# Splitting the weights of the projections beside the forgetting attention during the dense stage and keeping the two parts in DRAM

## The chip, the cores and the metric

One Trainium2 chip, one core. The metric is the device time of one launch in microseconds (us), the median of several runs. All matrix work is fp32 in and out.

## The reference

One residual block over 1024 tokens of width 1024. After an RMS norm a combined input projection feeds three token mixers: a gated linear recurrence (HGRN2), a forgetting attention (8 heads of 64 with a cumulative log-forget bias), and a cross-attention into 256 memory tokens. Three sigmoid gates of width 1024 weigh the three branches, one output projection closes the mixer, and a ConvGLU feed-forward layer follows. The lines that bear on the change:

```python
z = h @ w_in[l].astype(jnp.float32)
(hq, hf, hi, hg, fq, fk, fv, ff, mq, gate_logits) = jnp.split(z, pts, axis=-1)
y_a = _hgrn2_mixer(hq, hf, hi, hg, lower_bounds[l], hgrn_norm_g[l])
y_b = _fox_mixer(fq, fk, fv, ff, fox_f_bias[l], fox_q_norm_g[l], fox_k_norm_g[l])
...
y_c = _memory_mixer(mq, mem_kv, mem_q_norm_g[l], mem_k_norm_g[l])
gates = jax.nn.sigmoid(gate_logits).reshape(B, T, N_BRANCH, D_MODEL)
merged = (gates[:, :, 0] * (y_a @ w_br_hgrn[l].astype(jnp.float32))
          + gates[:, :, 1] * (y_b @ w_br_fox[l].astype(jnp.float32))
          + gates[:, :, 2] * (y_c @ w_br_mem[l].astype(jnp.float32)))
```

## The kernel before

**Split operands.** TensorE (PE) multiplies in a one-pass fp32 form (fp32r). To keep fp32 accuracy each operand is split in a high part, which is the value cast to fp32r, and a low part, which is the value minus the high part. A product then takes three matmuls (`mm3`, L248 to L250; in the attention stage L1229): high by high, high by low, low by high. The split of a weight tile is a cast on ScalarE (ACT, helper line L254) and a subtraction on VectorE (DVE, helper line L262, or L1216 in the attention stage). The raw weights come from DRAM into the tiles `raw` (two buffers) or `rw` (two buffers, dense stage); the parts lie in `wh` and `wl` (`WIDE` = 4 buffers each).

**Stages.** In the profile's time: start and memory keys (0 to 80 us); the dense stage (80 to about 250 us), in which 20 chunks of 128 output channels of the input projection (four for the memory queries, sixteen for gates) are made in ten pairs; values and first queries and keys of the attention, woven with the memory attention (to about 371 us); the attention stage (371 to 674 us); HGRN2; the merge and the output projection; the feed-forward layer from about 1000 us.

**Dense stage.** `dense_unit` makes one pair with seven block products instead of eight, from the four blocks a11, a21, a22, a12 of the pair's weights and their sums (L662). `Dense.open` issues the two loads of `rw` on GpSimd's queue (POOL, L684) when the unit begins and splits the first operands; `Dense.operand` makes each split on ACT and DVE. A tile scheduler puts the instructions of each engine in order ahead of time; on the chip each engine takes its own in that order. SP issues the stores of the gates (L770) and the loads of the tiles `raw`.

**Attention stage.** Here a planner, class `Plan`, writes the order of all engines out by hand: chains of work name an engine, a cost and the time from which they can start, and the planner takes the chain that can start first, lower rank first. `rows` makes logits and softmax (L1085, L1086, L1099, L1120), `outcomes` transposes the weights of attention, splits them (`ph`, `pl`, L254 and L1161) and multiplies with the values (L1171, L1172), `pairs` makes the next head pair's queries and keys. `fill`, with the lowest rank, fills PE with projections that have nothing to do with the attention heads at hand (L1229): first a job with the weights of head pair 1, then four parts of `w_late[0]` (queries and keys of head pairs 2 and 3), four gate chunks of `w_cm`, four parts of `w_late[1]` (HGRN2's inputs), and three chunks of `w_cm` for HGRN2's head 0. The 15 weight tiles of these last jobs, 128 x 1024 each, go through `stage_weights`: a load on SP's queue (L1207), then for each half a cast on ACT and a subtraction on DVE, as planned items between those of the attention:

```python
raw = wp.tile([P, 4 * 264], F32, tag="raw", name="raw", bufs=2)
t = yield "SP", 0.1, t
SP.dma_start(raw[:, :n], src[q] if count > 1 else src)
t += LOAD
...
for c in (slice(0, n // 2), slice(n // 2, n)):
    t = yield "ACT", act_us(n // 2), t
    cast(S, h[:, c], raw[:, c])
    t = yield "DVE", dve_us(n // 2), t + act_us(n // 2) + LAG
    V.tensor_sub(l[:, c], raw[:, c], h[:, c].bitcast(F32))
```

A slot of `wh` and `wl` comes free when the last matmul of an earlier job has read it (`ws.free`).

## Time and profile before

| | us |
|---|---|
| median of 3 runs | 1689.15 (1688.54 to 1690.55) |
| span of the profiled execution, first to last instruction | 1686.5 |
| the profiled execution's own time beside its span | not given apart; the median lies 2.6 above the span |
| PE busy | 1677.7 (99%) |
| DVE, ACT, POOL busy | 1170.4, 808.5, 326.6 |
| dense stage, 90 to 270: PE, DVE, ACT, POOL busy of 180 | 180.0, 102.4, 73.6, 7.5 |
| attention stage, 371 to 674: PE, DVE, ACT, POOL busy of 303 | 301.6, 226.7, 185.6, 143.4 |
| granted TensorE clock | 1.000 |

Matmuls are pipelined: one of 512 columns is listed with about 0.39 us but the next one starts 0.227 us later. So "busy" does not tell whether PE runs at its own pace; the distance from one matmul's start to the next does. In rows of the timeline the columns are start and duration in us, engine, line, operation, output and inputs, shape, count, and in brackets the engine's idle time before it and what ended it.

### The profile page before, as it was taken

What the parts mean: (1) busy time and instruction counts of PE and PEld (TensorE: products, weight loads), DVE (VectorE), ACT (ScalarE), POOL (GpSimd) and SP (SyncE); (2) the same over time, 40 slices, a digit from 0 to 9 for tenths busy, and PEclk for the clock granted to TensorE, in tenths of its full rate; (3) what the DMA queues carried; (4) which work ended last, traced back from release to release, by engine and by line L of the source; (5) the groups of instructions that cost most, each with busy time, mean ns of one, the idle gap of its engine ahead of it and who ended that gap; (6) DMA issues with size and microseconds to landing.
All of it is one profiled execution on the core that took longest, in us unless ns stands there. A gap on an engine that the chain in (4) does not pass through costs nothing.

```text
span 1686.5 us, 23254 instructions
## 1 busy us (share of the span) xinstructions
PE 1677.7 (99%) x8409; PEld 1415.8 (84%) x8409; DVE 1170.4 (69%) x2118; ACT 808.5 (48%) x1459; POOL 326.6 (19%) x430
## 2 busy tenths in 40 slices
PE   9999999999999999999999999999999999999999
PEld 7888889998888888888888888888888888888887
DVE  6966554558688766766856745988788888775664
ACT  6734444656576556666521333634344444533432
POOL 0200001336464423433201000211111111100000
PEclk9999999999999999999999999999999999999999
DMA  9442324122142233100337641666454454494782
GB/s 376 171 145 105 118 77 157 71 100 69 57 133 87 75 101 101 51 20 19 107 106 257 207 151 58 189 180 182 132 144 131 122 166 132 176 352 154 239 283 88
DMA packets 87348, 235.50 MB, mean 140 GB/s; under 512 B 9904, under 2 KB 12600, under 8 KB 87104
## 3 DMA queue, kind: packets, MB, share of 16 engines
q1 hardware_dynamic: 68032, 166.83, 28.4%
q0 software_dynamic: 18624, 66.59, 13.9%
q8 instruction: 66, 1.08, 0.3%
q10 hardware_dynamic: 576, 0.59, 0.1%
q14 instruction: 50, 0.41, 0.1%
HBM read 184.91 MB, written 72.13 MB: 152 GB/s over the span
## 4 chain that ended last, share of the span: by engine, by line
PE 96%; DVE 2%; ACT 1%; DMA 1%; issue 0%; ACTq 0%; DVEq 0%
PE pp L250 17%; PE pp L249 17%; PE pp L248 17%; PE pp L1229 10%; PE lg L248 5%; PE lg L250 5%; PE lg L249 5%; PE tr L250 3%; PE tr L249 3%; PE tr L248 3%; PE tr L1147 2%; PE po L1172 1%; PE lg L1085 1%; PE lg L1086 1%; PE po L248 1%; PE po L249 1%
## 5 line engine op out<-in xcount | busy, mean ns | idle before, releaser
L254 ACT CAST wh<-s 128x512 fp32r<-128x512 f32 x122 | 73.3, 620 | 133.1 <-PE pp L249 73.3
L254 ACT CAST wh<-rw 128x512 fp32r<-128x512 f32 x96 | 58.5, 619 | 113.8 <-PE pp L249 69.7
L254 ACT CAST wh<-raw 128x512 fp32r<-128x512 f32 (+2 forms) x85 | 63.9, 756 | 96.0 <-PE pp L249 76.3
L254 ACT CAST dwh<-wr 128x1024 fp32r<-128x1024 f32 (+1 forms) x41 | 40.2, 980 | 114.1 <-PE tr L249 37.6
L250 PE MATMUL pp<-uh,wl 128*128 128x512 f32 x224 | 89.0, 397 | 0.0
L248 PE MATMUL pp<-uh,wh 128*128 128x512 f32 x224 | 88.8, 396 | 0.0
L249 PE MATMUL pp<-ul,wh 128*128 128x512 f32 x224 | 88.4, 395 | 0.0
L1161 DVE TENSOR_TENSOR pl<-tr,ph 128x512 fp32r<-128x512 f32 (+1 forms) x96 | 51.4, 551 | 30.7 <-ACT ph L254 30.3
L1120 ACT ACTIVATE pt<-pt,st 128x128 f32<-128x128 f32 (+3 forms) x64 | 49.6, 775 | 45.9 <-DVE st L1116 30.6
L1229 PE MATMUL pp<-wl,uh 128*128 128x512 f32 (+1 forms) x192 | 70.0, 365 | 0.0
L1229 PE MATMUL pp<-wh,uh 128*128 128x512 f32 (+1 forms) x192 | 69.5, 362 | 0.0
L1229 PE MATMUL pp<-wh,ul 128*128 128x512 f32 (+1 forms) x192 | 69.4, 362 | 0.0
L262 DVE TENSOR_TENSOR dwl<-wr,dwh 128x1024 fp32r<-128x1024 f32 (+1 forms) x41 | 46.3, 1130 | 30.5 <-ACT dwh L254 30.5
L254 ACT CAST ph<-tr 128x512 fp32r<-128x512 f32 (+1 forms) x96 | 44.2, 477 | 41.0 <-PE tr L1147 39.6
L1124 POOL TENSOR_SCALAR pt<-pt,st 128x128 f32<-128x128 f32 (+3 forms) x64 | 52.0, 815 | 60.1 <-DVE st L1122 58.4
L1828 POOL DMA_DIRECT2D rw<-in_w_up x42 | 23.2, 558 | 200.0 <-DVE wl L1718 190.1
L1718 DVE TENSOR_TENSOR wl<-rw,wh 128x512 fp32r<-128x512 f32 x69 | 46.6, 687 | 21.2 <-PE pp L250 17.9
L1718 DVE TENSOR_TENSOR wl<-s,wh 128x512 fp32r<-128x512 f32 x85 | 57.9, 683 | 0.0
L262 DVE TENSOR_TENSOR wl<-raw,wh 128x512 fp32r<-128x512 f32 (+2 forms) x54 | 52.1, 964 | 7.0 <-ACT wh L254 7.0
L248 PE MATMUL pp<-wh,uh 128*128 128x256 f32 (+1 forms) x192 | 55.2, 287 | 0.0
L250 PE MATMUL pp<-wh,ul 128*128 128x256 f32 (+1 forms) x192 | 55.0, 286 | 0.0
L249 PE MATMUL pp<-wl,uh 128*128 128x256 f32 (+1 forms) x192 | 54.4, 283 | 0.0
(520 smaller groups left out, 5602.2 us busy)
## 6 DMA issues: line engine op xcount, KB each, us to landing
rw<-in_w_up POOLq DMA_DIRECT2D x42, 512.0 KB, 4.8
sd<-in_w_dn POOLq DMA_DIRECT2D x30, 512.0 KB, 6.0
br<-yd SPq DMA_DIRECT2D x30, 512.0 KB, 5.6
gd<-gt SPq DMA_DIRECT2D x48, 256.0 KB, 2.0
gt<-gd SPq DMA_DIRECT2D x48, 256.0 KB, 2.8
yd<-fc SPq DMA_DIRECT2D x44, 256.0 KB, 2.8
wr<-sd SPq DMA_DIRECT2D x20, 512.0 KB, 4.9
raw<-in_w_cm SPq DMA_DIRECT2D x18, 512.0 KB, 3.5
```

The lines of the kernel that those rows point to most:

```text
L248: PE.matmul(ps, lh, rh, start=first, stop=False, skip_group_check=more)
L249: PE.matmul(ps, lh, rl, start=False, stop=False, skip_group_check=more)
L250: return PE.matmul(ps, ll, rh, start=False, stop=last, skip_group_check=more)
L254: return S.copy(out, in_)
L262: return (sub or V).tensor_sub(l, src, h.bitcast(F32))
L1120: S.activation(pt, pt, AF.Exp, bias=st[:, 2:3], accum_out=st[:, 3:4])
L1124: G.tensor_scalar(pt, pt, st[:, 3:4], 0.0, ALU.mult, ALU.add)
L1147: PE.transpose(ptr[:, j * P:(j + 1) * P], pts[j][:, sb * P:(sb + 1) * P], ident)
L1161: V.tensor_sub(pl[:, c], ptr[:, c], ph[:, c].bitcast(F32))
L1229: PE.matmul(o, a, b, start=q == i == 0, stop=q == KC - 1 and i == 2)
L1718: late["split"] = V.tensor_sub(l, src, h.bitcast(F32))
L1828: late["raw"] = (SP if begun else G).dma_start(raw[:, 2 * i:2 * i + 2, :], src[:, 2 * i:2 * i + 2, :])
```

## The change

The 15 weight tiles of the projections in the attention stage are split earlier, in the dense stage, and both parts go to a DRAM tensor `wsd`. In the attention stage the two parts are loaded as they are.

- `stored_parts` is a generator that `dense_unit` advances four times in each unit but the first (at most one half tile each time). For each tile: the raw load on SP (L273), for each half a cast on POOL (L258, tile `piece`, two buffers in the places `ta` and `tb`), a subtraction on DVE that leaves the low part in `raw` (L262), a store of the high half (L743) and, after the second half, one of the low part (L745).
- `load_parts` issues two loads of 128 x 1024 on SP (L755), one into `wh`, one into `wl`. `stage_weights` only takes a free slot and calls it; the planner reckons with `LOAD` + 1.0.
- `Dense.load` issues a unit's weight loads on POOL (L678) one unit ahead, in the middle of the unit before, behind the last cast of a piece, and `open` uses what is there.
- In the dense stage and in the attention stage the scheduler and the planner come to another order on every engine; the numbers of instructions on PE and DVE stay as they were (8107 and 2120 in the program), ACT has 30 fewer, POOL 30 more, SP's queue 75 more.

```diff
+        def load(self, src):
+            self.ahead = self.raw()
+            for i in range(2):
+                G.dma_start(self.ahead[:, 2 * i:2 * i + 2, :], src[:, 2 * i:2 * i + 2, :])
+
         def open(self, src, places=None):
-            raw = []
-            whole = None if places else self.raw()
-            for i in range(2):
+            raw = [] if places else [self.ahead[:, i, :] for i in range(4)]
+            for i in range(2 if places else 0):
...
+    stored = [*((w_late, q) for q in range(4)), *((w_cm, 16 + 8 * br + j) for br, j in order[2 + NCOVER + NPAIR:]),
+              *((w_late, q) for q in range(4, 8)), *((w_cm, i) for i in (4, 0, 8))]
+    wsd = tc.dram_tile([len(stored), 2, P, T], F32, name="wsd")
+
+    def stored_parts():
...
+        fetch(0)
+        fetch(1)
+        yield
+        for i in range(len(stored)):
+            raw = raws.pop(i)[:, :T]
+            for n in range(2):
+                sl = slice(n * HB, (n + 1) * HB)
+                h = ps1.tile([P, HB], F32R, tag=("ta", "tb")[n], name="piece")
+                split(G, h, raw[:, sl].bitcast(F32R), raw[:, sl])
+                late["piece"] = late["split cast"]
+                SP.dma_start(wsd[i, 0][:, sl], h.bitcast(F32))
+                if n:
+                    SP.dma_start(wsd[i, 1], raw)
+                elif i:
+                    fetch(i + 1)
+                yield
+
+    def load_parts(i, shape):
+
+        n = shape[0] * shape[1]
+        hl = [wp.tile([P, 4 * 264], F32R, tag=g, name=g, bufs=WIDE) for g in ("wh", "wl")]
+        for c, t in enumerate(hl):
+            SP.dma_start(t[:, :n].bitcast(F32), wsd[i, c])
+        return [t[:, :n].rearrange("p (a b) -> p a b", a=shape[0]) for t in hl]
+
-    def dense_unit(src, put, first, families):
+    def dense_unit(src, put, first, families, spare, after):
...
         put(0, 1, y, e2)
+        next(spare, None)
+        if after is not None:
+            with tc.issue_after(late["piece"].ins) if "piece" in late else nullcontext():
+                dense.load(after)
...
-    ws, raws = Ring(WIDE, 2), Ring(2)
+    ws = Ring(WIDE, 2)
...
     def stage_weights(jobs):
-        for j, (src, shape, count) in enumerate(jobs):
+        at = 0
+        for j, (shape, count) in enumerate(jobs):
             parts[j] = []
             for q in range(count):
-                n = shape[0] * shape[1]
-                kr, t = yield from raws.get()
-                raw = wp.tile([P, 4 * 264], F32, tag="raw", name="raw", bufs=2)
-                t = yield "SP", 0.1, t
-                SP.dma_start(raw[:, :n], src[q] if count > 1 else src)
-                t += LOAD
-                kw, tw = yield from ws.get()
...
-                    cast(S, h[:, c], raw[:, c])
...
-                    V.tensor_sub(l[:, c], raw[:, c], h[:, c].bitcast(F32))
...
+                kw, t = yield from ws.get()
+                t = yield "SP", 0.2, t
+                parts[j].append((load_parts(at, shape), kw, t + LOAD + 1.0))
+                at += 1
```

**DVE at the passage from the first to the second dense unit, before.** `s1`, `s2`, `s3` and `s4` are block sums, `rw` the raw weights, `gt` evacuates a product from PSUM.

```order
L262 TENSOR_TENSOR wl_849<-s3_885,wh_848 128x512
L662 TENSOR_TENSOR s3_1003<-rw_923 128x512
L759 TENSOR_TENSOR gt_882<-lg_788,fe_845 128x512
L262 TENSOR_TENSOR wl_905<-rw_923,wh_904 128x512
L662 TENSOR_TENSOR s1_928<-rw_923 128x512
L662 TENSOR_TENSOR s2_934<-s1_928,rw_923 128x512
L757 SCALAR_TENSOR_TENSOR gt_901<-pp_787,fe_831 128x512
L262 TENSOR_TENSOR wl_931<-s1_928,wh_930 128x512
```

The same place now; `raw_1004` is the first of the 15 tiles.

```order
L262 TENSOR_TENSOR wl_850<-s3_889,wh_849 128x512
L662 TENSOR_TENSOR s3_1011<-rw_886 128x512
L807 TENSOR_TENSOR gt_883<-lg_789,fe_846 128x512
L262 TENSOR_TENSOR wl_909<-rw_886,wh_908 128x512
L262 TENSOR_TENSOR raw_1004<-raw_1004,piece_1030 128x512
L262 TENSOR_TENSOR raw_1004<-raw_1004,piece_1054 128x512
L662 TENSOR_TENSOR s1_929<-rw_886 128x512
L805 SCALAR_TENSOR_TENSOR gt_905<-pp_788,fe_832 128x512
L662 TENSOR_TENSOR s2_935<-s1_929,rw_886 128x512
L262 TENSOR_TENSOR wl_932<-s1_929,wh_931 128x512
```

Two subtractions, which wait for POOL's casts, now stand ahead of the sum `s1` and the low part `wl_932` that PE waits for.

**ACT in the attention stage before, where the second `w_late` group begins.** `ph` is a part of the transposed attention weights, `pt4` and `pt5` rows of the softmax, `kh` and `qa` keys and queries of the next head pair, `raw_5152` the group's first tile.

```order
L1000 ACTIVATE kh0_2_4872<-tr_5139,cv_71 64x512
L1000 ACTIVATE kh1_2_4873<-tr_5139,cv_71 64x512
L254 CAST ph_5174<-tr_5161 128x128
L254 CAST wh_5154<-raw_5152 128x512
L1120 ACTIVATE pt4_5178,st_5179<-pt4_5178,st_5179 128x640
L1186 COPY gt_5213<-po_5028 64x512
L1000 ACTIVATE qa0_2_4876<-tr_5210,fqs_185 64x512
```

ACT at the same keys and the same softmax row now.

```order
L1050 ACTIVATE kh0_2_5013<-tr_5286,cv_71 64x512
L1050 ACTIVATE kh1_2_5014<-tr_5286,cv_71 64x512
L1170 ACTIVATE pt4_5278,st_5279<-pt4_5278,st_5279 128x640
L254 CAST ph_5343<-tr_5317 128x384
L1317 ACTIVATE gt_5305<-gt_5305 128x512
L1170 ACTIVATE pt5_5329,st_5330<-pt5_5329,st_5330 128x768
```

The cast of the raw weights no longer stands between the keys and the softmax row.

**SP's queue in the attention stage, around the loads of the second `w_late` group and the gates' stores, before.** `gd` takes gates, `ybd` the attention's output, `z3_1` is a tile of queries and keys.

```order
L1281 DMA gd_197<-gt_5121 128x512
L1207 DMA raw_5152<-in_w_late 128x1024
L1321 DMA z3_1_5220<-zd_2248 128x4x256
L1192 DMA ybd_196<-gt_5213 64x512
L1281 DMA gd_197<-gt_5238 128x512
L1207 DMA raw_5367<-in_w_late 128x1024
```

The same part of the queue now; `wsd` holds the stored parts, and each load waits until PE has read the old content of its slot.

```order
L1319 DMA gd_197<-gt_5170 128x512
L755 DMA wh_5307<-wsd_706 128x1024
L755 DMA wl_5308<-wsd_706 128x1024
L1242 DMA ybd_196<-gt_5298 64x512
L1319 DMA gd_197<-gt_5305 128x512
L1359 DMA z3_1_5418<-zd_2414 128x4x256
```

Where one raw load (L1207) stood in SP's queue before, two loads of the same size stand now.

More of the change, by code (lines that the diff above doesn't have):

```diff
@@ L681, in open @@
                     t = t.rearrange("p (a b) -> p a b", a=2)
-                else:
-                    t = whole[:, 2 * i:2 * i + 2, :]
                 G.dma_start(t, src[:, 2 * i:2 * i + 2, :])
@@ L715, in tile_block, with fetch @@
     ps1 = home["sums"] = Rounded(tc, name="ps1", bufs=1, side="right", reuse_waits="tile")
-    def dense_unit(src, put, first, families):
+    stored = [*((w_late, q) for q in range(4)), *((w_cm, 16 + 8 * br + j) for br, j in order[2 + NCOVER + NPAIR:]),
+              *((w_late, q) for q in range(4, 8)), *((w_cm, i) for i in (4, 0, 8))]
+    wsd = tc.dram_tile([len(stored), 2, P, T], F32, name="wsd")
+    def stored_parts():
+        w_late_flat = [w_late[q // 4][q % 4] for q in range(8)]
+        raws = {}
+        def fetch(i):
+            if i < len(stored):
+                src, q = stored[i]
+                raws[i] = raw_weights(w_late_flat[q] if src is w_late else src[q], T)
+        fetch(0)
[21 more added lines that the diff above has]
+    def dense_unit(src, put, first, families, spare, after):
         raw, o1, o6, o2, s2, o3 = gen["unit"] if first else dense.open(src)
@@ L739, in dense_unit @@
         put(1, 1, x, e5)
+        next(spare, None)
         if not first:
@@ L743, in dense_unit @@
             put(0, 0, z, e1)
+            next(spare, None)
         product(x, dense.operand(a22), "T4", False)
         put(1, 0, x, None)
+        next(spare, None)
     def dense_put(chunks):
@@ L784, in tile_block @@
     run_all(cover)
+    spare = stored_parts()
     for i, chunks_of in enumerate(PAIRS):
-        dense_unit(w_pair[i], dense_put(chunks_of), i == 0, families)
+        dense_unit(w_pair[i], dense_put(chunks_of), i == 0, families, iter(()) if i == 0 else spare, w_pair[i + 1] if i + 1 < len(PAIRS) else None)
+    run_all(spare)
     home["raw"].release()
@@ L1199, in stage_weights @@
     def stage_weights(jobs):
-        for j, (src, shape, count) in enumerate(jobs):
+        at = 0
+        for j, (shape, count) in enumerate(jobs):
             parts[j] = []
             for q in range(count):
-                n = shape[0] * shape[1]
-                kr, t = yield from raws.get()
-                raw = wp.tile([P, 4 * 264], F32, tag="raw", name="raw", bufs=2)
-                t = yield "SP", 0.1, t
-                SP.dma_start(raw[:, :n], src[q] if count > 1 else src)
-                t += LOAD
-                kw, tw = yield from ws.get()
-                h, l = (wp.tile([P, 4 * 264], F32R, tag=g, name=g, bufs=WIDE) for g in ("wh", "wl"))
-                t = max(t, tw)
-                for c in (slice(0, n // 2), slice(n // 2, n)):
-                    t = yield "ACT", act_us(n // 2), t
-                    cast(S, h[:, c], raw[:, c])
-                    t = yield "DVE", dve_us(n // 2), t + act_us(n // 2) + LAG
-                    V.tensor_sub(l[:, c], raw[:, c], h[:, c].bitcast(F32))
-                    t += dve_us(n // 2) + LAG
-                raws.free(kr, t)
-                parts[j].append(([x[:, :n].rearrange("p (a b) -> p a b", a=shape[0]) for x in (h, l)], kw, t))
+                kw, t = yield from ws.get()
+                t = yield "SP", 0.2, t
+                parts[j].append((load_parts(at, shape), kw, t + LOAD + 1.0))
+                at += 1
     def three(ps, lh, ll, rh, rl):
@@ L1340, in tile_block @@
     gates = list(islice(early, NFOX))
-    sources = [(w_late[0], (2, HB), 4)] + [(w_cm[16 + 8 * order[i][0] + order[i][1]], (KC, P), 1) for i in gates]
-    sources += [(w_late[1], (2, HB), 4), *((w_cm[i], (KC, P), 1) for i in (4, 0, 8))]
+    sources = [((2, HB), 4), *[((KC, P), 1)] * NFOX, ((2, HB), 4), *[((KC, P), 1)] * 3]
     zr.update({(0, 0): 0.0, (0, 1): 7.0})
```

## The prediction

> **What bounds the kernel now.** I read the page's head first, then the windows of the two stages that the change touches, then PE's timeline in them.
>
> ```profile
> span 1686.5 us, 23254 instructions
> ...
> PE 1677.7 (99%) x8409; PEld 1415.8 (84%) x8409; DVE 1170.4 (69%) x2118; ACT 808.5 (48%) x1459; POOL 326.6 (19%) x430
> ```
>
> ```profile
> 90.00:270.00 180.00, 180.00 (x821) 150.10 (x820) 102.39 (x159) 73.56 (x128) 7.51 (x14) 1.00 0.30 105
> 371.00:674.00 303.00, 301.63 (x1661) 256.35 (x1661) 226.67 (x683) 185.63 (x384) 143.36 (x184) 1.00 0.29 95
> ```
>
> The columns of a window are its length, then PE, PEld, DVE, ACT and POOL busy, the granted clock, the DMA share and GB/s. PE has no idle time in the dense stage and 303.00 - 301.63 = 1.37 us in the attention stage, at a granted clock of 1.00. Busy alone proves little where a matmul is listed longer than its turn; the starts prove it:
>
> ```profile
> 177.01 0.39 PE L250 MATMUL tr<-uh,wl 128*128 128x512 f32 x1
> 177.24 0.39 PE L248 MATMUL tr<-uh,wh 128*128 128x512 f32 x1
> 177.47 0.39 PE L249 MATMUL tr<-ul,wh 128*128 128x512 f32 x1
> ```
>
> Matmuls of 512 columns follow each other every 0.23 us. The change leaves PE's instructions as they are, so it can only win where that distance is longer. In the attention stage these are the places where PE waits:
>
> ```profile
> 503.24 0.40 PE L1229 MATMUL pp<-uh,wl 128*128 128x512 f32 x1
> 504.02 0.50 PE L1085 MATMUL lg<-kh,qa 128*128 128x512 f32 x1 [0.38 <-DVE st L1099]
> ...
> 504.60 0.39 PE L1229 MATMUL pp<-uh,wh 128*128 128x512 f32 x1
> 505.13 0.41 PE L1085 MATMUL lg<-kh,qa 128*128 128x384 f32 x1
> ...
> 507.58 0.40 PE L1229 MATMUL pp<-uh,wh 128*128 128x512 f32 x1
> 508.09 0.50 PE L1085 MATMUL lg<-kh,qa 128*128 128x512 f32 x1
> ```
>
> ```profile
> 516.76 0.28 PE L1171 MATMUL po<-ph,vhl 128*128 128x256 f32 x1
> 517.57 0.39 PE L1172 MATMUL po<-pl,vhl 128*128 128x256 f32 x1 [0.53 <-DVE pl L1161]
> ```
>
> Less the turn (0.23, or 0.12 for 256 columns) they cost 0.55, 0.30, 0.28 and 0.69 us: **1.82 us** together. Three shorter ones stand earlier:
>
> ```profile
> 398.35 0.39 PE L1229 MATMUL pp<-wh,ul 128*128 128x512 f32 x1
> 398.87 0.30 PE L1085 MATMUL lg<-kh,qa 128*128 128x128 f32 x1
> ...
> 400.77 0.39 PE L1229 MATMUL pp<-wl,uh 128*128 128x512 f32 x1
> 401.13 0.50 PE L1085 MATMUL lg<-kh,qa 128*128 128x512 f32 x1
> ```
>
> ```profile
> 424.42 0.40 PE L1229 MATMUL pp<-wh,ul 128*128 128x512 f32 x1
> 424.90 0.63 PE L1147 MATMUL tr<-ident,pt 128*128 128x128 f32 x4
> ```
>
> They cost 0.29, 0.13 and 0.25 us. So all waits of this stage come to 2.5 us. After it I find two more that are worth naming, in HGRN2 and in the feed-forward layer:
>
> ```profile
> 695.79 0.22 PE L1511 MATMUL lg<-X 128*64 128x64 f32 x1
> 696.73 0.74 PE L1523 MATMUL lg<-X 128*128 128x64 f32 x5 [0.72 <-DVE X L1501]
> ```
>
> ```profile
> 1070.27 0.39 PE L249 MATMUL pp<-B11l,wh 128*128 128x512 f32 x1
> 1071.02 0.50 PE L250 MATMUL pp<-B11h,wl 128*128 128x512 f32 x1 [0.36 <-DVE wl L1718]
> ```
>
> By the starts, less a turn, they cost 0.83 and 0.52 us. With them the whole reserve behind the first matmuls is 2.5 + 1.35 = 3.85 us, 0.23% of the time.
>
> **What ends the waits.** The chain of waits goes from the matmuls of 504 to 508 us back through DVE and ACT to one load, and ACT's timeline shows it standing:
>
> ```profile
> 495.25 6.32 DMA raw<-in_w_late
> ```
>
> ```profile
> 501.60 0.62 ACT L254 CAST wh<-raw 128x512 fp32r<-128x512 f32 x1 [3.00 <-DMA raw<-in_w_late]
> ```
>
> ACT sits 3.00 us in front of the cast of a weight that PE does not need for a long time; the softmax row and the keys behind it are late, then DVE, then PE. The wait at 517.57 has another source of the same work:
>
> ```profile
> 515.05 2.13 DVE L1216 TENSOR_TENSOR wl<-raw,wh 128x512 fp32r<-128x512 f32 x2
> ```
>
> Two subtractions of weights stand ahead of `pl` and take 2.13 us together instead of about 1.3.
>
> **The change, removed.** From ACT's and DVE's order in the attention stage go 30 casts and 30 subtractions:
>
> ```profile
> L1216 DVE TENSOR_TENSOR wl<-raw,wh 128x512 fp32r<-128x512 f32 x30 | 22.6, 759 | 1.9 <-ACT wh L254 1.8
> ```
>
> That is 22.6 us of DVE's 226.7; the 30 casts at the 0.62 us of the row at 501.60 are 18.6 us of ACT's 185.6. On a stage that PE sets, this is worth nothing in itself: 303 us of PE turns stay. What goes with it is the cause of the four waits: neither ACT nor DVE meets a weight load any more. I take 1.82 us, with the bounds 0 (other lateness takes the same places) and 2.5 (every wait of the stage goes).
>
> **Moved to the dense stage.** 30 casts on POOL. The nearest row has the same shape:
>
> ```profile
> L258 POOL TENSOR_SCALAR vhl<-Vf x8: 620/622/1586, 375.8 to 597.5; 128x512 fp32r<-128x512 f32 x8
> ```
>
> 30 x 0.62 = 18.6 us on an engine with 7.5 of 180 us busy. The 30 subtractions at about 0.69 us, the duration of the rows below, are 20.7 us more on DVE, 102 + 21 = 123 of 180. What covers it is the lead that the splits have over PE:
>
> ```profile
> 168.44 0.69 DVE L262 TENSOR_TENSOR wl<-rw,wh 128x512 fp32r<-128x512 f32 x1
> ```
>
> This low part is ready at 169.13, and the first matmul that reads its tile is the one at 177.01: 7.9 us of lead. A unit of 7 x 12 matmuls lasts 84 x 0.227 = 19 us and takes four subtractions, 2.8 us, or 4.3 at the slow price of 515.05. The lead holds. It was not used up by late loads either, which DVE already meets:
>
> ```profile
> DVE s L662 <- DMA rw<-in_w_pair: 12.0, 6, 3.5
> ```
>
> Six waits of 2 us on average for `rw`, and PE lost nothing. These loads are now issued half a unit earlier, though behind the casts on POOL's queue; queued behind POOL's issue are only the next casts. Cost 0, bounds 0 and 2 us: at the passage to the second unit the lead is smaller.
>
> ```profile
> 90.33 0.68 DVE L262 TENSOR_TENSOR wl<-s,wh 128x512 fp32r<-128x512 f32 x1
> ```
>
> ```profile
> 95.42 0.39 PE L250 MATMUL lg<-T1h,wl 128*128 128x512 f32 x1
> ```
>
> 95.42 - 91.01 = 4.4 us, and the changed order puts two subtractions ahead, 1.4 us: 3.0 remain. If POOL's casts come 3 us late there, since they wait for a raw load, the cover is gone and each further microsecond is PE's.
>
> Something speaks against the move. The two subtractions at 515.05 ran beside POOL's work on the softmax, and each took about 1.07 us; in the dense stage POOL has been idle so far, and now its casts run beside DVE. That is where the slow price above is from, and why the dense stage has a chance of its own below, though 4.3 us in a unit stay under the lead of 7.9. [...]
>
> **Added: loads that PE itself waits for.** Before, a weight went load, cast, subtraction; now PE waits for two loads behind SP's queue. The price of one is seen at the raw loads of the stage (L1207):
>
> ```profile
> L1207 SPq DMA_DIRECT2D raw<-in_w_late x8: 328/382/424, 373.3 to 539.6; - x8
> ...
> DMA to landing us min/median/max: 3.1/3.7/7.0
> ```
>
> SP takes 0.38 us for an issue, so the second load of a pair follows that far behind. How much time they have I count in the changed order of PE, as the matmuls between the last reader of a slot's old content and the first reader of the new, at turns of 0.23 us for 512 columns, 0.12 for 256 and 0.11 for a transpose: 5.4 us for the first of HGRN2's three chunks, 6.7, 8.1, 8.4 and 8.5 at four other passages from job to job, over 20 for the remaining ten. A pair at the median lands after about 0.4 + 3.7 + 0.4 = 4.5 us; cost 0. At the maximum of 7.0 it is 7.8: 2.4 + 1.1 = 3.5 us if it struck both tightest places. I take 0.2 us, near the median. Behind the waiting loads in SP's queue stand stores of `zd`, `ybd` and `gd`, as they stood behind the raw loads before; their tiles have three buffers. In the dense stage SP issues 15 loads and 45 stores more, 60 x 0.38 = 23 us in some 150, in front of gates whose tiles are asked for again only three stores later.
>
> **Sum.** Against the execution's own span: 1686.5 - 1.82 + 0 + 0.2 = 1684.9, and with the 2.6 us by which the median lies above the span, **1687.5 us**.
>
> **Rivals.**
> - *New waits of the same size.* The planner counts on fixed durations and closes up the order as soon as ACT and DVE have room, so PE's margins to `lg`, `tr` and `pl` may be as thin as before, and HGRN2's ACT and DVE are also put in another order. For it: the three early waits are not all of this kind. Against it: the four large ones have a named cause. Time 1689.2.
> - *PE stands at the weight loads.* One mechanism, at the five passages. It decides from where a pair needs more than 7 us, since (7 - 5.4) + (7 - 6.7) = 1.9 eats the gain. At 9.5 us it costs 4.1 + 2.8 + 1.4 + 1.1 + 1.0 = 10.4: 1687.3 + 10.4 = 1697.7, slower. For it: 6.32 us at 495.25 and the maximum of 7.0, for single loads. Against it: the median of 3.7, and a DMA share of 0.29 in the stage.
> - *The dense stage stalls* at the passage to the second unit, or because DVE stands in front of a cast that is late. 2 us at that passage: 1689.5.
> - *Everything goes*, the waits of the attention stage and those at 696 and 1071 too, which the change does not touch: 1689.15 - 3.85 = 1685.3, faster.
>
> **How the numbers follow.** This kernel's runs lie within 0.12% of each other, and I call less than 0.2%, 3.4 us, no change. The forecast has 0.52, new waits 0.23, loads that PE stands at 0.10 (a fifth of that under 3.4 us), a stalled dense stage 0.08 (a quarter of it with more than 3.4), everything 0.07. Slower is 0.08 + 0.02 = 0.10, faster 0.07, the same 0.83. The forecast's own range is 1686.6 to 1688.5; to hold 8 in 10 it goes from 1685.8, between the forecast and the full reserve, to 1690.8.
>
> **What would show it.** In the profile after: ACT's row of waits for `raw` in the attention stage is gone; PE's starts near 500 to 520 us keep 0.23 apart; PE idle there under 1 us; PE busy 180.0 of 180 in the dense stage although DVE is at about 123; POOL's `piece` casts near 0.62 us. Wrong would be PE rows of L1267 with a wait that ends at a DMA of `wsd`, or PE idle between 85 and 100 us. If the time falls under 1685.3, turns themselves got shorter, which nothing here explains.

## The result: 9 us slower, and where they went

| | before | after |
|---|---|---|
| median of 5 runs, us | 1689.25 (1688.54 to 1690.55) | 1698.41 (1696.90 to 1700.66) |
| ratio after to before, 95% interval | | 1.0053 (1.0042 to 1.0065) |
| span of the profiled execution, us | 1686.5 | 1697.7 |

The change makes the kernel 0.5% slower. The prediction was 1687.5 us, with a range that ended at 1690.8 and a chance of 0.10 for slower.

The chain that ended last, by engine, first on the page of before and then on that of after:

```profile
PE 96%; DVE 2%; ACT 1%; DMA 1%; issue 0%; ACTq 0%; DVEq 0%
```

```profile
PE 91%; DMA 5%; DVE 2%; ACT 1%; issue 1%; POOL 0%; SPq 0%; ACTq 0%; DVEq 0%; POOLq 0%
```

PE's work is the same, but the chain now leaves PE for about 9% of the span instead of 4%, and most of what is new is DMA. The windows of the two stages in after (length, PE, PEld, DVE, ACT, POOL busy, clock, DMA share, GB/s):

```profile
90.00:270.00 180.00, 174.22 (x758) 142.48 (x757) 122.87 (x185) 67.70 (x121) 28.75 (x42) 0.99 0.69 232
371.00:674.00 303.00, 301.90 (x1696) 259.10 (x1695) 206.88 (x651) 166.99 (x344) 138.39 (x183) 1.00 0.34 117
```

In the dense stage PE has 180 - 174.22 = 5.78 us of idle time, where it had none. DVE's 122.87 is what was predicted (123). The attention stage has 1.10 us idle instead of 1.37: the work left it, PE's idle time hardly did.

From here on **loss** means the time between the first and the last matmul's start in 85 to 270 us, less one turn for every matmul listed in between, in the one profiled execution of a kernel. It is 0.16 us before and 8.9 after: the 5.78 idle, 0.15 us of each wait that the row of the matmul ahead hides (at 156.22 in after 2.48 us lie between two starts, of which 2.10 are listed as idle and 0.23 are a turn), and turns of 0.43 us in place of 0.227. It builds up late:

```profile
125.00:145.00 20.00, 20.00 (x90) 16.57 (x89) 14.68 (x22) 6.35 (x13) 4.90 (x7) 1.00 0.92 296
145.00:165.00 20.00, 17.78 (x70) 13.88 (x69) 14.02 (x22) 7.04 (x14) 3.97 (x6) 0.91 0.88 306
165.00:185.00 20.00, 18.07 (x80) 14.64 (x79) 15.38 (x23) 6.23 (x12) 5.17 (x9) 1.00 0.85 288
```

Until 145 us nothing is lost; from there PE idles 2.22, 1.93, 0.09 and 1.54 us in four slices of 20 us, while DVE is busy 13 to 15 of the 20 only. So DVE is late without being full. The chain that ends at the first long wait says what it stands for:

```profile
140.17 8.50 DMA wsd<-raw
...
148.73 4.33 DMA raw<-in_w_late
...
153.23 0.62 POOL piece L258
...
153.88 0.62 DVE raw L262
...
155.57 0.61 DVE gt L811
156.18 0.04 issue
156.22 0.50 PE pp L248
```

DVE's own timeline at that place:

```profile
153.88 1.69 DVE L262 TENSOR_TENSOR raw<-raw,piece 128x512 fp32r<-128x512 f32 x2 [2.75 <-POOL piece L258]
155.49 0.68 DVE L811 TENSOR_TENSOR gt<-pp,fe 128x512 f32<-128x512 f32 x1
```

The store of a low part takes 8.50 us to land, only then can the raw buffer be loaded again (4.33), POOL casts, and DVE, which has stood 2.75 us in front of this low part, subtracts. Behind the two low parts in DVE's order is the evacuation (L811) that gives PE its tile `pp` back (the program's PSUM tiles `pp`, `lg`, `tr` and `po` take PE's products). PE has waited 2.10 us for it. DVE's order in the program of after, a unit earlier, shows how the low parts stand (number in the order, line, instruction; those between are left out):

```
129 L262 TENSOR_TENSOR raw_1080<-raw_1080,piece_1192
131 L262 TENSOR_TENSOR raw_1080<-raw_1080,piece_1218
133 L807 TENSOR_TENSOR gt_1001<-lg_938,fe_981
136 L262 TENSOR_TENSOR raw_1196<-raw_1196,piece_1243
137 L262 TENSOR_TENSOR raw_1196<-raw_1196,piece_1328
138 L805 SCALAR_TENSOR_TENSOR gt_1027<-pp_937,fe_965
139 L807 TENSOR_TENSOR gt_1051<-tr_1034,fe_951
145 L262 TENSOR_TENSOR raw_1247<-raw_1247,piece_1357
146 L262 TENSOR_TENSOR raw_1247<-raw_1247,piece_1385
149 L262 TENSOR_TENSOR raw_1361<-raw_1361,piece_1408
150 L262 TENSOR_TENSOR raw_1361<-raw_1361,piece_1493
151 L811 TENSOR_TENSOR gt_1156<-lg_1093,fe_1138
```

The scheduler draws the low parts forward, as far as it believes their data is there: twelve of them precede `gt_1156`, in front of which the program's text, whose order the numbers in the names follow, has three (pieces 1030, 1054 and 1076). From the first low part of the first tile to that of the 15th, 14 tiles on, the order passes 19 evacuations on DVE, and ACT does two more in that stretch. At four to a unit these 21 are 5.25 units, 5.25 x 19.05 = 100.0 us, or 7.1 us a tile. POOL's first casts of a tile, however, start between 86.8 and 199.0 us: 112.2 / 14 = 8.0 us a tile. DVE's order asks for tiles faster than they come, and the difference, 12 us over the 14 tiles, eats up DVE's lead over PE.

The waits in the dense stage of after, 85 to 270 us:

```profile
POOL piece L258 <- DMA raw<-in_w_late: 26.5, 3, 11.1
...
POOL piece L258 <- DMA raw<-in_w_cm: 20.1, 3, 7.0
DVE raw L262 <- POOL piece L258: 19.3, 9, 4.7
DVE s L662 <- DMA rw<-in_w_pair: 18.9, 5, 6.0
```

### The profile page after: what moved, and what is told of

It is laid out like the page before. It is cut to its first block, busy times and chain, and to the rows that moved or that the text cites. A ratio compares the mean times of both kernels' runs of the same rounds, so it can differ in the third digit from the quotient of the medians.

```text
span 1697.7 us, 23407 instructions
## 1 busy us (share of the span) xinstructions
PE 1681.9 (99%) x8409; PEld 1418.4 (84%) x8409; DVE 1180.1 (70%) x2118; ACT 791.8 (47%) x1429; POOL 347.2 (20%) x460
## 3 DMA queue, kind: packets, MB, share of 16 engines
q0 software_dynamic: 18624, 66.59, 14.3%
q8 instruction: 66, 1.08, 0.3%
## 4 chain that ended last, share of the span: by engine, by line
PE 91%; DMA 5%; DVE 2%; ACT 1%; issue 1%; POOL 0%; SPq 0%; ACTq 0%; DVEq 0%; POOLq 0%
PE pp L248 16%; PE pp L249 16%; PE pp L250 16%; PE pp L1267 10%; PE lg L248 4%; PE lg L250 4%; PE lg L249 4%; PE tr L248 3%; PE tr L249 3%; PE tr L250 3%; PE tr L1197 2%; DMA wsd<-raw 1%; PE po L1222 1%; PE lg L1136 1%; PE po L248 1%; PE lg L1135 1%
## 5 line engine op out<-in xcount | busy, mean ns | idle before, releaser
L254 ACT CAST wh<-raw 128x512 fp32r<-128x512 f32 (+2 forms) x55 | 45.7, 832 | 83.1 <-PE pp L249 70.4
L262 DVE TENSOR_TENSOR dwl<-wr,dwh 128x1024 fp32r<-128x1024 f32 (+1 forms) x41 | 46.3, 1130 | 31.1 <-ACT dwh L254 31.1
L262 DVE TENSOR_TENSOR wl<-raw,wh 128x512 fp32r<-128x512 f32 (+2 forms) x54 | 52.1, 964 | 7.9 <-ACT wh L254 7.8
L248 PE MATMUL pp<-T4h,wh 128*128 128x512 f32 x128 | 51.0, 398 | 5.7 <-DVE gt L811 5.6
L817 ACT ACTIVATE gt<-gt 128x512 f32<-128x512 f32 x32 | 20.2, 632 | 77.9 <-issue 39.5
```

The source lines that it names most:

```text
L248: PE.matmul(ps, lh, rh, start=first, stop=False, skip_group_check=more)
L254: return S.copy(out, in_)
L262: return (sub or V).tensor_sub(l, src, h.bitcast(F32))
```

## The experiments

The runs of the kernel before that stood beside these ones have medians of 1688.8 to 1689.4 us; each ratio goes against those on the same chip. The theories in the expectations:

- **A**: DVE stands in its order in front of low parts whose casts wait for raw loads; evacuations behind them are late.
- **B**: the transfers by themselves make the unit loads `rw` late.
- **C**: SP's order holds up the gates' stores.
- **D**: the time of 30 more DVE instructions, and what POOL's casts beside them add to it (two subtractions beside POOL's work took about 1.07 us each at 515.05 in before, others 0.69).
- **F**: casts that wait on POOL hold up the unit loads behind them in its queue.
- **G**: A, with its cause: the order draws low parts far ahead of their places and asks for tiles faster than the loads bring them.

| run | median, us | ratio (95%) | loss, us |
|---|---|---|---|
| the change | 1698.41 | 1.0053 (1.0042 to 1.0065) | 8.9 |
| 1 attention stage alone | 1689.56 | 1.0005 (0.9995 to 1.0015) | 0.13 |
| 2 transfers alone | 1689.88 | 1.0007 (0.9998 to 1.0017) | 0.13 |
| 3 no stores | 1699.20 | 1.0060 (1.0045 to 1.0075) | 8.6 |
| 4 low part on POOL | 1703.72 | 1.0091 (1.0076 to 1.0106) | 12.3 |
| 5 resident weights | 1697.17 | 1.0046 (1.0031 to 1.0061) | 3.9 |
| 6 casts on ACT | 1698.49 | 1.0057 (1.0042 to 1.0072) | 8.0 |
| 7 low part one piece later | 1697.50 | 1.0050 (1.0033 to 1.0067) | 6.6 |
| 8 low part in its own tile | 1693.31 | 1.0021 (1.0012 to 1.0030) | 4.6 |
| 9 low parts pinned | 1701.35 | 1.0076 (1.0061 to 1.0091) | 9.4 |
| 10 pinned, own tile | 1692.25 | 1.0020 (1.0011 to 1.0029) | 3.2 |
| 11 pinned, resident | 1689.68 | 1.0007 (0.9998 to 1.0017) | 0.18 |
| 12 half the tiles | 1689.08 | 1.0007 (0.9997 to 1.0016) | 0.11 |
| 13 pinned, own tile, loads first | 1698.88 | 1.0059 (1.0043 to 1.0076) | 9.5 |
| 14 pinned, loads first | 1706.80 | 1.0105 (1.0090 to 1.0120) | 14.3 |
| 15 loads first | 1692.01 | 1.0017 (1.0008 to 1.0027) | 2.1 |
| 17 loads first, own tile | 1688.70 | 1.0003 (0.9994 to 1.0012) | 0.13 |
| 18 pinned, own tile, loads two ahead | 1690.16 | 1.0008 (0.9999 to 1.0017) | 0.13 |

### Run 1: the attention stage alone, and run 16: the kernel before once more

```diff
-        for i in range(len(stored)):
+        for i in range(1):
...
-            SP.dma_start(t[:, :n].bitcast(F32), wsd[i, c])
+            SP.dma_start(t[:, :n].bitcast(F32), wsd[0, c])
...
```

> Left out: only the first of the 15 weight tiles is split and stored in the dense stage, and the attention stage loads this one pair of parts 15 times (its projections get wrong weights); the unit loads are issued as before. So the attention stage is that of the change and the dense stage nearly that of before. All theories agree on the dense stage: PE back to under 0.5 us of loss there. The prediction's own term for the attention stage says 1.8 us less than before, reduced to 1.5 by what the profile of the change shows: 1689.25 - 1.5 = 1687.7, range 1686.8 to 1688.6. If the loss of 1.76 us at 913 us (merge, DVE evacuation L1696) comes from the new order of the attention stage, it is here too and the time is 1689.5; if it comes from the dense stage or is chance, it is not.

> The kernel before, unchanged, for a second profile. If the wait of DVE L1659 for gate loads near 903 us stalls PE here too, by 0.5 us or more, it is the spread of one kernel and not the change. If PE again loses nothing there, it belongs to the new order. Time 1689 +- 2.

Run 1 puts the whole loss of time into the dense stage, but the attention stage gives nothing back: 1689.56, and 1 lies inside the interval. Run 16 (1688.21 us, a single time) says why. Its PE row of the attention stage, and PE and ACT where the prediction had its three waits at 504 to 508 us:

```profile
371.00:674.00 303.00, 302.26 (x1673) 257.87 (x1672) 227.14 (x684) 186.58 (x385) 143.20 (x184) 1.00 0.30 95
```

```profile
504.42 0.39 PE L1229 MATMUL pp<-uh,wl 128*128 128x512 f32 x1
504.65 0.40 PE L1085 MATMUL lg<-kh,qa 128*128 128x512 f32 x1
504.89 0.39 PE L1086 MATMUL lg<-kl,qa 128*128 128x512 f32 x1
505.12 0.40 PE L1229 MATMUL pp<-uh,wh 128*128 128x512 f32 x1
505.35 0.34 PE L1085 MATMUL lg<-kh,qa 128*128 128x384 f32 x1
```

```profile
501.30 0.62 ACT L254 CAST wh<-raw 128x512 fp32r<-128x512 f32 x1 [1.52 <-DMA raw<-in_w_late]
```

The same program, and the three waits are not there: matmuls 0.23 apart, ACT stands 1.52 us instead of 3.00 for the same load. They belonged to one of the two executions. Of the four waits only the one at 517 us is in both (0.53 us, at 517.26 in run 16). PE idles 1.37 and 0.74 us there in the two profiles of before, 1.10 with the change, and 1.0 to 2.3 in the six runs that lose nothing in the dense stage (1, 2, 11, 12, 17 and 18; 1.25 in run 1): no gain to be had.

The merge stage, 860 to 930 us, in before (run 16 reads the same, 70.00), in after and in run 12:

```profile
860.00:930.00 70.00, 70.00 (x322) 58.02 (x321) 44.06 (x68) 14.45 (x24) 9.43 (x17) 1.00 0.61 198
```

```profile
860.00:930.00 70.00, 68.41 (x314) 56.12 (x313) 40.24 (x64) 14.72 (x27) 10.95 (x18) 1.00 0.58 184
```

```profile
860.00:930.00 70.00, 69.93 (x320) 57.60 (x319) 42.67 (x66) 14.25 (x23) 9.88 (x17) 1.00 0.61 197
```

Run 1 idles 0.84 us here. PE waits for an evacuation (L1696 in after) that waits for a gate load `gt<-gd`; these land in up to 8.5 us in after and 6.6 in before. Both profiles of before have none of it, and all 17 of changed kernels have 0.07 to 1.86 us of idle time here. That it comes with the new order is likely from that; by which instruction was not tried.

### Runs 2, 3, 5, 11: transfers without the work, work without the transfers

Run 2 stores the raw weights instead of the parts; run 3 leaves the stores out; run 5 also takes the raw loads away; run 11 is run 5 with each low part pinned behind the gate evacuated last in the program's text.

```diff
 run 2
-                split(G, h, raw[:, sl].bitcast(F32R), raw[:, sl])
-                SP.dma_start(wsd[i, 0][:, sl], h.bitcast(F32))
+                SP.dma_start(wsd[i, 0][:, sl], raw[:, sl])
 run 5
-            raw = raws.pop(i)[:, :T]
+            raw = raws[i % 2][:, :T]
...
 run 11, 9 and 10: pinned
+                with tc.issue_after(late["put"].ins):
                     split(G, h, raw[:, sl].bitcast(F32R), raw[:, sl])
```

> Left out: the split itself. The raw loads go on, and the stores too, with the same number, size and place in SP's order, but they store the raw weights twice; POOL casts nothing and DVE subtracts nothing in the dense stage. Theory A (DVE stands in its order in front of the low parts, whose casts on POOL wait for raw loads, and PSUM evacuations behind them are late): the waits near 156 and 179 us go, about 6 of the 8.9 us lost in the dense stage, 1698.4 - 6 = 1692 at most, down to 1688 if late unit loads cost nothing either. Theory B (the transfers alone, at 0.9 DMA share, make the loads rw late and DVE's sums with them) and theory C (SP's order delays the gates' stores and their buffers): the loss stays, 1696 to 1699; B shows it as DVE waits L662 for rw, C as ACT or DVE waits for stores of gd.

> Left out: all stores of parts but those of tile 0; the attention stage loads that one pair 15 times (wrong weights). Raw loads, casts on POOL and subtractions on DVE go on. Two thirds of the added bytes are gone, and a raw buffer is free as soon as the subtraction has read it. Theory A in the form that the raw load is late because it waits for the store of the low part: casts are on time, DVE does not stand, 8 of the 8.9 us go, 1689.5 or less. [...]

> Left out: raw loads after the first two and stores after the first tile; the same two raw tiles are cast on POOL and subtracted on DVE again and again (wrong weights, the attention stage loads one pair 15 times as in the run without stores). All 30 casts and 30 subtractions stay, but none can wait for a transfer. [...] Theory A (DVE stands in its order in front of subtractions whose casts wait for raw loads) and theory F (casts that wait for raw loads on POOL hold the unit loads rw behind them): the loss goes to under 1 us, 1689.5, range 1688.5 to 1691.

> Left out: raw loads after the first two and stores after the first tile (as in the run with resident weights; wrong weights), with each low part pinned to its place. Theory G: the 3.9 us that the resident run lost came from low parts packed into 105 to 145 us, where DVE was busy 20.00 of 20 us; spread, the same 30 instructions cost under 0.5 us, 1689 to 1690, with DVE busy at most 17 of 20 us in each slice behind 105. Theory D (the DVE time itself): the loss stays at 3 to 4 us, 1693 to 1697.

Run 2 in the dense stage:

```profile
90.00:270.00 180.00, 180.00 (x814) 149.84 (x813) 103.04 (x163) 73.94 (x128) 7.47 (x14) 1.00 0.67 240
```

240 GB/s, a little more than in after, and PE loses 0.13 us: B and C fall as causes by themselves. Run 3 has the loss without the stores, against my expectation for A, which I had tied to the store ahead of the raw load. With fewer transfers ahead, the scheduler draws the low parts forward still more: counted as above, 14 tiles stand within 2.75 units, 3.7 us a tile, and come every 4.9. In run 5, where no cast waits for a load, the low parts are crowded in until DVE itself is full:

```profile
105.00:125.00 20.00, 20.00 (x89) 16.50 (x88) 20.00 (x27) 6.84 (x13) 12.43 (x15) 1.00 0.36 123
125.00:145.00 20.00, 16.80 (x73) 13.29 (x72) 19.48 (x27) 5.41 (x10) 10.65 (x14) 1.00 0.22 67
```

This is a miss for A as I had put it (under 1 us of loss) and for D, which I had put at 6 to 9 us of loss, though the median of 1697.17 lies in the range that I had given D (1695 to 1699); the profiled execution, with a span of 1693.5, is a short one of that kernel. Run 11 decides: the same 30 casts and 30 subtractions at the same engines, spread as the program's text has them, leave a loss of 0.18 us.

```profile
90.00:270.00 180.00, 180.00 (x820) 150.06 (x819) 123.61 (x190) 76.47 (x129) 32.83 (x42) 1.00 0.34 117
```

So neither the work nor the transfers cost anything by themselves; what costs is the order in which the work stands to the transfers.

### Runs 4, 6, 7, 8: other engines, other tile

```diff
 run 4
-                split(G, h, raw[:, sl].bitcast(F32R), raw[:, sl])
+                split(G, h, raw[:, sl].bitcast(F32R), raw[:, sl], G)
 run 6
+                split(S, h, raw[:, sl].bitcast(F32R), raw[:, sl])
 run 7: the subtraction of a piece stands in the generator's next step
 run 8
+                lo = ps1.tile([P, HB], F32R, tag=("la", "lb")[n], name="low")
+                split(G, h, lo, raw[:, sl])
...
```

> Nothing left out: the low parts are subtracted on POOL, behind the casts on the same engine, instead of on DVE. All transfers stay. Theory A: DVE no longer stands in front of pieces; what remains is the lateness of rw: 1698.4 - 6 = 1692, and 1690 if that costs little. Theories B and C: 1696 to 1699 as with the change. Theory D predicts a gain of the DVE time (20 us) but only a part of the loss: 1693 to 1696. POOL needs about 30 x (0.62 + 1.1) = 52 us, the subtraction's 1.1 us being an estimate from the two subtractions beside POOL's work that took 1.07 us each; if it is slower than 2 us the pieces get late and the parts are stored later, without touching PE.

> Nothing left out: the casts of the pieces go from POOL to ACT; POOL's queue then holds only the unit loads, as before the change. Theory F: rw loads are issued in time, waits of L662 for rw fall to about the 12 us of before, and the loss falls to 3 us or less, 1692. Theory A: ACT now stands in front of the late raw loads and DVE behind ACT, so the loss stays or grows: 1697 to 1702, with ACT rows of piece that wait for raw. Theory D: without POOL beside DVE a part of the loss goes, 1694 to 1696.

> Nothing left out: each low part is subtracted one step of the generator later than its cast (a quarter of a unit, about 5 us), so that DVE meets it when the cast has had that much time. Loads and casts stay on their queues, raw buffers come free one step later. Theory A: DVE no longer stands in front of pieces (19.3 us of waits for POOL with the change, here under 5) and at least half of the 8.9 us goes: 1692 to 1694. Theory F: rw loads stay as late as with the change or get later, loss stays, 1697 to 1700. Theory D: 1697 to 1699.

> Nothing left out: the low part goes into a tile of its own (two places of 128 x 512) and is stored in halves, so a raw buffer is free when the subtraction has read it and not when the store of the low part has landed; 15 stores more on SP. If the store ahead of the raw load (SP waited 23.5 us for it) is what makes the casts late, the loss falls by half or more: 1692 to 1694. If the landing of the raw load by itself (2.6 to 11.3 us) under the added traffic is enough, as the run without stores suggests, it stays: 1696 to 1699.

Run 4 lost more, against every theory's figure. A subtraction on POOL takes 1.30 us (estimated 1.1), and the chain before its longest wait, 6.4 us at 179.6, shows a second way in which a late raw load reaches DVE:

```profile
158.71 4.61 DMA raw<-in_w_late
163.51 0.60 POOL piece L258
164.11 0.19 issue
164.30 0.46 POOL rw L678
164.90 6.05 DMA rw<-in_w_pair
```

The unit load waits in POOL's queue behind the cast that waits for the raw load. That is F, and run 6 tests it in the other direction, with nothing but unit loads on POOL:

```profile
DVE raw L262 <- ACT piece L254: 23.2, 10, 7.4
...
DVE s L662 <- DMA rw<-in_w_pair: 12.1, 6, 4.9
```

DVE's waits for `rw` are those of before (12.0), and the loss stays at 8.0: in the change F is not needed, A is enough. With the casts off POOL the longest low part `wl` from `rw` takes 0.693 us, against 1.095 in after, and 0.9 us less is lost; that is the most that run 6 leaves for what POOL's casts add to DVE's instructions, unless the casts cost something on ACT. Run 7 missed its aim: the scheduler drew the delayed low parts forward just as far, and DVE still waited 18.1 us for POOL. Run 8, where a raw buffer is free without waiting for a store, halves the loss as expected for the store's share (1692 to 1694).

### Runs 9, 10, 13, 14: pinned low parts, and a loop of my own making

```diff
 run 13, 14: at the start of dense_unit, not in its middle
+        if after is not None and not first:
+            with tc.issue_after(late["piece"].ins) if "piece" in late else nullcontext():
+                dense.load(after)
...
```

In runs 13, 14 and 18 the casts also stand behind the unit load of their own unit.

> Nothing left out: each low part is put behind the DVE instruction of the gate that was evacuated last in the program, so that the scheduler cannot draw it forward. Theory G (the scheduler fills DVE's idle time with low parts far ahead of their places in the program, eight of them in front of one evacuation; the lead of the splits is used up, and whatever comes late then is PE's): at least two thirds of the 8.9 us go, dense stage under 3 us, 1691 to 1692.5. Theory A (not the place but the late raw loads make DVE stand): low parts still wait for POOL and the raw loads, loss 6 to 10 us, 1696 to 1700.

> Nothing left out: the low part in a tile of its own, as in the run that measured 1693.3, and pinned to its place as in the run beside this one. Theory G: dense stage under 1.5 us, 1690 to 1691. Theory A: as without the pins, 4 to 5 us in the dense stage, 1693 to 1694.

> Nothing left out: as the run with pinned low parts in a tile of their own (1692.3, 3.2 us lost in the dense stage), and the unit loads are issued at the start of a unit instead of at its first place for pieces, about 11 us earlier, ahead of the unit's casts on POOL. Theory G with F (both the low parts drawn forward and the unit loads behind waiting casts): dense stage under 0.5 us, 1689.5, range 1688.5 to 1690.5, as the attention stage alone gave 1689.6. A third cause: 2 to 4 us remain, 1692 to 1693.

> Nothing left out: pinned low parts, in place in the raw tile as in the change, and the unit loads at the start of a unit. Against the run with pins alone (1701.4, 9.4 us lost) only the place of the unit loads differs. Theory G with F: under 1 us in the dense stage, 1689.5 to 1690.5; waits of DVE and ACT for rw back to some 12 us. If the store ahead of the raw load keeps the casts late enough to hold the unit loads still, 2 to 4 us, 1692 to 1694.

None of the four reached what theory G gave. Run 10 came nearest (1692.25 for 1690 to 1691; its profiled execution, of 1696.05 us, was the longest of ten). The 9.4 us of run 9 lie in the range for A, but not for A's reason: its waits show that the pins did what they should and something else broke:

```profile
DVE s L662 <- DMA rw<-in_w_pair: 42.4, 11, 6.2
ACT wh L254 <- DMA rw<-in_w_pair: 33.5, 7, 6.0
```

DVE waits for POOL 0.2 us in all, but both engines now wait for the unit loads. POOL's timeline in run 13:

```profile
155.75 0.62 POOL L258 TENSOR_SCALAR piece<-raw 128x512 fp32r<-128x512 f32 x1 [4.69 <-DMA raw<-in_w_cm]
156.31 1.11 POOL L678 DMA_DIRECT2D rw<-in_w_pair  x2
...
176.72 0.62 POOL L258 TENSOR_SCALAR piece<-raw 128x512 fp32r<-128x512 f32 x1 [4.57 <-DVE low L262]
177.53 1.12 POOL L678 DMA_DIRECT2D rw<-in_w_pair  x2 [0.18 <-issue]
```

Cast, low part behind its evacuation, buffer free, raw load, next cast, unit load, sums, evacuation: the pins close this into a ring, and its turn (156.31 to 177.53, and 20.2 us on average to 216.83) is longer than a unit's 19.05. By itself that says only that ring and stage move together, since the evacuation in the ring waits for PE; that the ring sets the pace is shown by run 18 below, which opens it. Runs 13 and 14 had been meant to free the unit loads, but moved them by one cast only, which is not out of the ring.

### Runs 12, 15, 17, 18: without the debt

```diff
 run 12: eight tiles, a piece at every second place
-        for i in range(len(stored)):
+        for i in range(8):
...
 run 15: unit loads at the start of a unit (as above) and its casts behind them
+                with tc.issue_after(late["unit load"].ins):
                     split(G, h, raw[:, sl].bitcast(F32R), raw[:, sl])
 run 17: run 15 with the own tile of run 8
 run 18: run 10 with each unit load two units ahead
```

> Left out: only eight of the 15 tiles are split and stored, a piece at every second place, and the attention stage loads these eight for all 15 (some projections get wrong weights). Not pinned. Half the traffic, POOL and DVE work. If the loss goes with the amount, 4 to 5 us in the dense stage, 1693 to 1694. Theory G: the scheduler still draws the low parts forward, but two raw buffers and the distance of the places bound how many, 1 to 3 us, 1690.5 to 1692.5. Theory A: each late piece costs as before, 4 to 5 us.

> Nothing left out: the change with the unit loads issued at the start of a unit and the casts behind them, no pins. Theory G with F: the low parts are still drawn forward as far as the casts allow; those are now held behind the unit load of their own unit, so fewer of them can stand in front of an evacuation: half of the loss, 4 to 5 us, 1693 to 1694. If F alone were the cause in the change: under 1 us, 1690. If G alone: 7 to 9 us, 1697.

> Nothing left out: the change with the unit loads at the start of a unit (2.1 us lost in the dense stage) and the low part in a tile of its own (4.6 us lost by itself). If the loss is a debt of DVE's order against late raw loads, both together leave under 0.7 us: median 1690, range 1689 to 1691.3, the rest over the kernel before being the waits for gate loads in the merge stage (1 to 1.7 us). If something else costs PE in the dense stage, 2 us or more stay there and the median is 1692 or more. Either way no gain over the kernel before: a second profile of it shows only one of the attention stage's four long waits, so there is nothing of size to win.

> Nothing left out: low parts pinned and in a tile of their own, as in the run that lost 9.5 us, with each unit load issued two units ahead as soon as its buffer's last reader is in the program, one cast earlier on POOL (some 5 us). If the unit loads behind the serial chain of casts are what cost there (cast, low part, evacuation, raw load, cast, unit load: about 21 us a turn against 19 of a unit), 5 us more lead leave under 2 us lost, 1690.5 to 1692. If the pinned low parts themselves make the evacuations late, the loss stays at 8 to 10 us, 1697 to 1699.

Run 12 has its 16 low parts at the same places of DVE's order as after has its first 16; the last cast is at 141 us, and it loses 0.11, less than any theory gave: the debt ends before the lead is used up. That fits after, which loses nothing until 145 us. In run 15 a cast cannot pass the unit load of its own unit; by the same count 28 low parts now stand over 6.5 units and not over 5.25, 4.3 in a unit against 5.3 or 8.8 us a tile against 7.1, and 2.1 us are left, which lies between the figures for F alone and for both together. Run 17, which adds the own tile, in the dense stage:

```profile
90.00:270.00 180.00, 180.00 (x815) 149.87 (x814) 127.14 (x192) 73.92 (x128) 28.74 (x42) 1.00 0.70 239
```

PE is busy 180.00 of 180 with all 15 tiles split and stored, 239 GB/s, and DVE busier than in after. The unit loads come earlier in this run too, but DVE still waits 16.3 us for `rw` (18.9 in after), so F is not what went; its waits for POOL's casts fall from 19.3 to 7.6 us:

```profile
DVE s L662 <- DMA rw<-in_w_pair: 16.3, 7, 3.3
...
DVE low L262 <- POOL piece L258: 7.6, 7, 1.6
```

G is shown: less asked per unit and earlier buffers, and the whole loss goes. Each of the two alone leaves a part (2.1 us in run 15, 4.6 in run 8). Run 18 takes the unit loads out of the ring by issuing them two units ahead, and there too the loss goes (from 9.5 in run 13 and 3.2 in run 10). Neither is faster than before: the median of run 17 is 1688.70, ratio 1.0003 (0.9994 to 1.0012).

## Why the prediction was wrong, step by step

- **Dense stage "Cost 0, bounds 0 and 2 us": the step that failed.** The durations held at the median (casts 0.622 us against 0.62, low parts 0.680 against 0.69). DVE's 122.87 against 123 is partly chance: eight low parts took longer (below), and four other instructions no longer fell into the window. The mistake was to cover them by the lead of 7.9 us once per unit, as if each unit began with the lead anew. A low part that DVE stands for takes lead away, the next unit starts with less, and after three units it is gone. I compared work with free time (123 of 180) where I should have compared two paces: the low parts in DVE's changed order, 7.1 us a tile, which could be read beforehand, with the turn of a raw buffer (store, load, cast, subtraction), 8.0 us a tile, which I should have estimated from landings. The term put at 0 measured 8.7 us.
- **"60 x 0.38 = 23 us in front of gates".** I priced SP's issues and not the landing of the raw load behind a store in the same buffer. That is 8.50 + 4.33 us in the chain at 156 us; run 8 shows about half of the loss hanging on the store.
- **The slow price of a subtraction beside POOL's work**, about 1.07 us at 515.05 in before: the trace of after agrees that there is a price, of 0.41 us. Eight of the 30 low parts ran beside a cast, for 0.55 us, and took 1.08 or 1.09 us, the other 22 had none beside them and took 0.68 or 0.69.

```profile
137.80 1.28 DVE L262 TENSOR_TENSOR raw<-raw,piece 128x512 fp32r<-128x512 f32 x2
141.55 1.70 DVE L262 TENSOR_TENSOR raw<-raw,piece 128x512 fp32r<-128x512 f32 x2 [2.48 <-POOL piece L258]
```

  The pair of low parts at 137.80 has no cast beside it (1.28 us), the pair at 141.55 has one (1.70). The pair at 153.88 is of the second kind (1.69), so 0.41 of the 2.10 us at 156.22 are of this kind. It was not what decided: run 6 loses 8.0 us without POOL's casts, run 17 nothing with them.
- **The rival "dense stage stalls"** named the right instruction, "DVE stands in front of a cast that is late", but had it as one wait of 2 us at the passage to the second unit; it was a sum over units, and nothing was lost at that passage (PE 20.00 of 20 until 145 us). Its price was too small by a factor of four, and with it the range and the chance of slower.
- **Attention stage "1.82 us": wrong in size and in kind.** Three of the four waits (1.13 us) were those of one execution. The fourth, blamed on two weight subtractions, stays without them: 

```profile
520.96 0.22 PE L1221 MATMUL po<-ph,vhl 128*128 128x128 f32 x1
521.65 0.33 PE L1222 MATMUL po<-pl,vhl 128*128 128x128 f32 x1 [0.47 <-DVE pl L1211]
```

  So the rival "new waits of the same size" describes this stage. ACT's waits for `raw` did go, as predicted; that was worth nothing.
- **Loads that PE waits for, +0.2 us: the price was right, its reason is not shown.** The loads of `wsd` land in 3.2 to 9.1 us, median 5.4, slower than the 3.7 I had reckoned with, and no instruction waits for them. Five pairs were complete only 7.0 to 9.6 us after their first issue, more than the two tightest of the counted margins (5.4 and 6.7 us). Whether they stood at these passages is not shown, so that nothing was paid may be luck.
- **Waits that the change does not touch:** the one at 696 us (0.83) stands in both profiles of before and in none of the 17 of changed kernels, which have another order there; the one at 1071 stays (1081.5 us in after, 0.52); and the merge stage has the new one of up to 1.86 us, which takes what the first gives back, or more. None of this was in the sum.

By the same counting of starts, after has 8.7 us more than before in the dense stage, about 2 more behind 860 us (1.8 of it the wait in the merge stage), 1.5 more ahead of 85 us and 1.5 less in the attention stage. The last two are spread between executions as far as two profiles of one kernel can tell: run 16, the kernel before, has 1.2 more at the start and 1.3 less in the attention stage as well. The two spans differ by 11.2 us, the medians by 9.2: the profiled execution of before was the shortest of its five (1688.54 us), that of after one of its longer ones (1699.48).

## What to carry to other kernels

When work is put into another engine's idle time, compare paces and not sums: how many of the new instructions the changed order asks for per unit, against how many the buffer turn (store, load, cast, subtract) can bring. In this case a lead hid the difference once, not in every unit. In after two low parts for which DVE stood 2.75 us were ahead of the evacuation that gave PE its tile back, and PE waited 2.10 us; in run 4 a cast that waited for a raw load was ahead of a unit load on POOL. So look in the changed order of each engine for an instruction whose data can be late, and for what stands behind it. Before counting a wait of some tenths as a gain, look at a second execution of the kernel before.

## What the runs showed of the hardware

Here a wait of PE of about 2 us or more mostly cost more than its length. After the 2.10 us at 156.22 in after, PE's turns are 0.43 us instead of 0.227 for seven matmuls:

```profile
156.22 0.50 PE L248 MATMUL pp<-T4h,wh 128*128 128x512 f32 x1 [2.10 <-DVE gt L811]
...
157.08 0.63 PE L248 MATMUL pp<-T4h,wh 128*128 128x512 f32 x1
157.50 0.63 PE L249 MATMUL pp<-T4l,wh 128*128 128x512 f32 x1
157.93 0.63 PE L250 MATMUL pp<-T4h,wl 128*128 128x512 f32 x1
```

The window from 145 to 165 us has a granted clock of 0.91, that from 156.96 to 160.37 one of 0.50, and 7 x 0.2 = 1.4 us are lost beside the wait. The waits of 1.93 us at 178.89 and of 1.54 at 219.19 in after were followed by turns of 0.23. In the slices of 20 us from 85 to 265 us the lowest granted clock went with PE's longest wait: 0.83 to 0.91 in after and the seven runs with one of 2.1 to 6.4 us (3, 4, 6, 7, 8, 13 and 14), 0.91 in run 9 (1.9 us), 1.00 in runs 5 and 15 (1.7 and 1.5 us). But run 14 also has a slice, from 245 to 265 us, with 2.33 us of idle time and a clock of 1.00. What decides whether slow turns follow was not shown.

The landing of the same load also moved with what else was under way: unit loads took 5.2 us at the median in before, 7.4 in after, and 6.8 in run 2, whose traffic cost PE nothing.
